# Memory layer of a two-layer decoder step: row maxima read back from device memory, one transpose for both column blocks of the sample, keys' transposes in another PSUM pool

## The chip, the cores and the metric

The kernel runs on one core of one Trainium2 chip, in float32 and in its TensorE form float32r. The metric is the device time of one execution in microseconds (us). Engines are called by the profile's short names: PE is TensorE (PEld its weight load), DVE is VectorE, ACT is ScalarE, POOL is GpSimd, SP is SyncE, which here issues every DMA.

## The reference

One inference step of a trunk of two layers, on a prompt of 256 tokens and a sample of 8 sequences of 8 new tokens, 320 tokens in all, with width 1024. Layer 0 is a spatial-gating MLP, layer 1 an mLSTM (matrix memory) with 8 heads; each is followed by a gated MLP. The change lies in the mLSTM layer. Cut to what matters there, per head:

```python
b = jnp.cumsum(fc, axis=-1)                                   # log forget gates
D = b[..., :, None] - b[..., None, :] + ic[..., None, :]      # masked to s <= t
inter = b + m[..., None]
m_t = jnp.maximum(inter, jnp.max(D, axis=-1))                 # running maximum, one row per head
w_intra, w_inter = jnp.exp(D - m_t[..., None]), jnp.exp(inter - m_t)
sc = jnp.einsum('bhtd,bhsd->bhts', qc, kc) * w_intra
num = w_inter[..., None] * jnp.einsum('bhtd,bhde->bhte', qc, C) + jnp.einsum('bhts,bhse->bhte', sc, vc)
den = w_inter * jnp.einsum('bhtd,bhd->bht', qc, n) + jnp.sum(sc, axis=-1)
h = num / jnp.maximum(jnp.abs(den), jnp.exp(-m_t))[..., None]
...
C_new = decay[..., None, None] * C + jnp.einsum('bhsd,bhse->bhde', kg, vc)
...
hn = ((h - mu) * lax.rsqrt(var + EPS)).reshape(bsz, s, D_B) * gn_g
y = (jax.nn.sigmoid(o_pre) * hn) @ w_out
```

A head has keys and queries of width 128 and values of width 256, that is two blocks of 128 columns.

## The kernel before

Activations lie transposed, with features on the partitions and the 320 tokens along the free dimension. A block of 128 output features is 24 matmuls of 320 columns for a depth of 1024: each weight is split into a rounded high part `wh` and the rest `wl`, the activations likewise, and three of the four products are summed (`chunk`, `block`). A block's 512 KB of weights come by one DMA on SP's queue into a tile `raw` (four buffers, loaded up to four blocks ahead, line 127); ACT casts `wh` (line 154), DVE subtracts to get `wl` (line 155).

**The memory layer** (`layer_b`, from line 635) first makes the gates of all heads (`gates`): per head a row of 392 numbers in `Xf` (320 running maxima, 64 weights of the old state, 8 decays), whose last part is an `Exp` on ACT (line 725). `X` holds the rows as a high part on partitions 0 to 7 and the rest on 32 to 39 (lines 726, 727). Then come the heads in a loop from line 1057. One turn `h` of the loop contains the six weight blocks of head `h` (query, key, two value blocks, two output gate blocks) and, between them, the work of head `h` and the tail of head `h - 1`:

- `inter` and `numer` (h - 1): products with the old state and with the values, into PSUM tiles `num`.
- `stats` (h - 1): mean and variance per token; the normalised result goes to `hn`, three token blocks (128, 128, 64) by 256 columns, one ACT instruction for each.
- `state_prompt`, `state_sample` (h - 1): the new state `C`, with the decays in `dec`, stored from SP.
- `scores` (h): a matmul of `X` with a selector (`sel`, one 128 x 128 matrix for each head) puts head h's row on all 128 partitions, in the PSUM tile `pMb`; ACT makes the weights `w` from it, POOL masks them, DVE makes `Pf`, and from `qw` the operand `Qz`.
- `o_epi` (h): an output gate block is scaled (`o_b`, line 995) and its tanh taken (`th_o`).
- `finish` (h - 1): for each of the two column blocks `e`, three transposes of `hn` into a PSUM tile `phn`, a product with the gate (`y_b`, line 1009), and its split into `yhb` and `ylb`, the operands of the output projection.
- `k_nat`, `v_nat` (h): transposes of keys (`pk`) and values (`pv`) into PSUM, then scaled and split (`kgs`, `kgh`, `kgl`).

Some blocks of the output projection are computed inside the loop (`EARLY_OUT`, turns 4 to 6), the rest after it. After the loop the last head's `numer`, `stats`, two gate blocks and `finish` come, then the remaining projection.

**What sets the order.** PE's instructions are kept in the order of the program (`pin`). The other engines' order, and that of SP's queue, is fixed at build time by the framework's scheduler from the program's order and its own estimates; on the chip each engine runs its list in order. PSUM has eight banks: `psm` with three, which the weight blocks take in turn (with one of the two tiles of `state_sample` in most heads), and `psa` with five for everything else. A tile waits for the readers of the one that held its bank before.

Of the kernel before, what the change touches and what calls it, by code (L numbers as in the profile page):

```python
# [10 lines left out]
F32 = mybir.dt.float32  # L11
# [5 lines left out]
P = 128  # L17
# [8 lines left out]
NH = 8  # L26
# [11 lines left out]
class Net:  # L38
# [596 lines left out]
    def layer_b(self):  # L635
# [5 lines left out]
        with ExitStack() as ctx:  # L641
# [3 lines left out]
            gnh = lp.tile([P, 16], F32, name="gnh")  # L645
            colsT = lp.tile([P, 3, 96], F32, name="cols")
            X = lp.tile([P, 392], F32R, name="X")
            sel = lp.tile([P, NH, P], F32R, name="sel")
            mk = lp.tile([P, NB], F32, name="mk")
            mo = lp.tile([8, 9], F32, name="mo")  # L650
            pads = []
# [9 lines left out]
            def gates(rp):  # L661

                bif = rp.tile([40, 1 + NB], F32, name="bif")
                rst = rp.tile([40, 2, T], F32, name="rst")
                selr = rp.tile([P, NH, P], F32, name="selr")
                RS = rp.tile([P, 384], F32, name="RS")
                nc.sync.dma_start(bif, I["b_if"])
                nc.sync.dma_start(rst, I["seg"])
# [54 lines left out]
                nc.vector.tensor_tensor(seg(wi[:, :64]), m0.unsqueeze(2).to_broadcast([8, NB, NS]), seg(M[:, TP:]), op=SUB)  # L723
                nc.vector.tensor_tensor(wi[:, 64:72], m0, ML, op=SUB)
                nc.scalar.activation(Xf[:, T:392], wi, AF.Exp)
                nc.vector.tensor_copy(X[0:8], Xf)
                nc.vector.tensor_tensor(X[32:40], Xf, X[0:8].bitcast(F32), op=SUB)
                nc.vector.tensor_scalar(gnh, self.vecs[:, V_GN:V_GN + 16], 0.5, None, op0=MULT)
# [54 lines left out]
            def v_epi(h, j, ps):  # L783
# [2 lines left out]
                nc.scalar.copy(vT[:, T:384], ps[:, TP:T])  # L786
                S[h].setdefault("vT", []).append(vT)

            def scores(h):
                s = S[h]  # L790
                q, qh, ql = s["q"]
                k, kh, kl = s["k"]
                pb = self.psa.tile([P, 512], F32, tag="pa", name="pMb")
                sc = self.psa.tile([P, 512], F32, tag="pa", name="psc")
                if h:
                    mm(pb[:, :392], sel[:, h, :], X, True, True)
                mm3(sc[:, :TP], kh, kl, qh, ql, True, True)
                mm(sc[:, TP:384], k[:, P:TP], q[:, P:TP], True, True)
                mm(sc[:, 384:448], k[:, TP:384], q[:, TP:T], True, True)
                if not h:  # L800

                    mm(pb[:, :392], sel[:, h, :], X, True, True)
                w = hp.tile([P, 448], F32, tag="w", name="w", bufs=1)
                for (n, o, c0, c1, t) in ((P, 0, 0, TP, 0), (P, TP, P, TP, 1), (64, 384, TP, T, 2)):
                    nc.scalar.activation(w[:n, o:o + c1 - c0], pb[:n, c0:c1], AF.Exp, scale=-1.0, bias=colsT[:n, t, h:h + 1])
                for o in (0, TP):
                    nc.gpsimd.affine_select(w[:, o:o + P], w[:, o:o + P], pattern=[[1, P]], compare_op=ALU.is_ge, fill=0.0,
                                            base=0, channel_multiplier=-1)
                w3 = seg(w[:64, 384:448])
                nc.gpsimd.affine_select(w3, w3, pattern=[[-NS, NB], [0, NS]], compare_op=ALU.is_ge, fill=0.0, base=0,  # L810
                                        channel_multiplier=1)
                nc.gpsimd.affine_select(w3, w3, pattern=[[NS, NB], [1, NS]], compare_op=ALU.is_ge, fill=0.0, base=0,
                                        channel_multiplier=-1)
                dec = hp.tile([P, NB], F32, tag="dec", name="dec", bufs=2)
                nc.vector.tensor_copy(dec, pb[:, 384:392])
                qw = hp.tile([P, 64], F32, tag="qw", name="qw", bufs=1)
                nc.vector.scalar_tensor_tensor(qw, q[:, TP:T], 0.5, pb[:, T:384], op0=MULT, op1=MULT)
                Qd = Qz.rearrange("p (b e) -> p b e", e=136)
                nc.scalar.copy(Qd[:, :, 0:8], seg(qw))
                nc.vector.tensor_tensor(Qd[:, :, 64:72], seg(qw), Qd[:, :, 0:8].bitcast(F32), op=SUB)  # L820
                Pf = hp.tile([P, 448], F32, tag="Pf", name="Pf", bufs=1)
                Ph = hp.tile([P, 384], F32R, tag="Ph", name="Ph", bufs=1)
                Pl = hp.tile([P, 384], F32R, tag="Pl", name="Pl", bufs=1)
                nc.vector.scalar_tensor_tensor(Pf[:, :384], sc[:, :384], 0.25 * KSC, w[:, :384], op0=MULT, op1=MULT)
                nc.vector.scalar_tensor_tensor(Pf[:64, 384:], sc[:64, 384:448], 0.25 * KSC, w[:64, 384:], op0=MULT, op1=MULT)
                self.split(Ph[:, :384], Pl, Pf[:, :384])
                self.split(Ps[:64, :64], Ps[:64, 64:], Pf[:64, 384:])
                parts = self.parts
                nc.scalar.copy(Ps[64:], Ps[:64])
                self.parts = parts  # L830
                s["P"] = (Ph, Pl, dec)
# [23 lines left out]
            def k_nat(h):  # L855
                s = S[h]
                ks = s["k"][0]
                pk = self.psa.tile([P, 512], F32, tag="pa", name="pk")
                for t in range(3):
                    self.tr(pk[:, t * P:(t + 1) * P], ks[:, t * P:(t + 1) * P], self.ident)  # L860
                kgh = hp.tile([P, 2, P], F32R, tag="kgh", name="kgh", bufs=1)
                kgl = hp.tile([P, 2, P], F32R, tag="kgl", name="kgl", bufs=1)
                kgs = hp.tile([P, 2, P], F32R, tag="kgs", name="kgs", bufs=1)
                kgz = hp.tile([P, NB, P], F32R, tag="kgz", name="kgz", bufs=1)
                g = colsT[:, 2, 32 + h:33 + h]
                src = pk[:, 2 * P:3 * P]

                for i, (r, o) in enumerate(((slice(0, 32), slice(32, 64)), (slice(32, 64), slice(0, 32)))):
                    nc.scalar.activation(kgs[:, i, :], src, AF.Copy, scale=g)
                    nc.vector.scalar_tensor_tensor(kgs[o, i, :], src[r], g[r], kgs[r, i, :].bitcast(F32), op0=MULT, op1=SUB)  # L870
                s["kg"] = (kgh, kgl, kgs, kgz)
                if h < NH - 1:
                    k_mask(h)
                for t in range(2):
                    g = colsT[:, t, 32 + h:33 + h]
                    src = pk[:, t * P:(t + 1) * P]
                    nc.scalar.activation(kgh[:, t, :], src, AF.Copy, scale=g)
                    nc.vector.scalar_tensor_tensor(kgl[:, t, :], src, g, kgh[:, t, :].bitcast(F32), op0=MULT, op1=SUB)
# [52 lines left out]
            def stats(h, between=None):  # L931
# [25 lines left out]
                made = nc.vector.scalar_tensor_tensor(nb, mv[:, :, 0], -1.0, sl, op0=MULT, op1=MULT)  # L957
                if between:
                    self.pin(made)
                for t in range(3):  # L960
                    n = P if t < 2 else 64
                    if h == NH - 1 and t:
                        nc.vector.tensor_scalar(hn[:n, t, :], src[t][:n, :DV], mv[:n, t, 0:1], sl[:n, t:t + 1], op0=SUB, op1=MULT)
                    else:
                        nc.scalar.activation(hn[:n, t, :], src[t][:n, :DV], AF.Identity, scale=sl[:n, t:t + 1], bias=nb[:n, t:t + 1])

            def state_prompt(h):
                s = S[h]
# [24 lines left out]
            def o_epi(h, j, ps):  # L993
                o = lp.tile([P, T], F32, tag="ob", name="o_b", bufs=1)
                nc.vector.tensor_tensor(o, ps[:, :T], self.rb, op=MULT)  # L995
                th = lp.tile([P, T], F32, tag="tho", name="th_o", bufs=4)
                nc.scalar.activation(th, o, AF.Tanh, scale=0.5)
                S[h].setdefault("o", []).append(th)

            def finish(h):  # L1000
                s = S[h]
                yh = hp.tile([P, 2, T], F32R, tag="yhb", name="yhb", bufs=6)
                yl = hp.tile([P, 2, T], F32R, tag="ylb", name="ylb", bufs=6)
                for e in range(2):
                    pt = self.psa.tile([P, 512], F32, tag="pa", name="phn")
                    for t in range(3):
                        self.tr(pt[:, t * P:(t + 1) * P], hn[:, t, e * P:(e + 1) * P], self.ident)
                    y = self.tp.tile([P, T], F32, tag="yf", name="y_b", bufs=2)
                    nc.vector.scalar_tensor_tensor(y, s["o"][e], 1.0, pt[:, :T], op0=ADD, op1=MULT)
                    g = gnh[:, 2 * h + e:2 * h + e + 1]  # L1010
                    nc.scalar.activation(yh[:, e, :], y, AF.Copy, scale=g)
                    nc.vector.scalar_tensor_tensor(yl[:, e, :], y, g, yh[:, e, :].bitcast(F32), op0=MULT, op1=SUB)
# [12 lines left out]
            vb = hp.tile([P, CW], F32R, name="vb")  # L1025
            Qz = hp.tile([P, 8 * 136], F32R, name="Qz")
            Ps = hp.tile([P, P], F32R, name="Ps")
            hn = hp.tile([P, 3, DV], F32, name="hn")
            nc.gpsimd.memset(hn[64:, 2, :], 0.0)
            nc.gpsimd.memset(vh[:, :, DV:DV + 1].bitcast(F32), 1.0)  # L1030
            nc.gpsimd.memset(vh[:, :, DV + 1:].bitcast(F32), 0.0)
            nc.gpsimd.memset(vl[:, :, DV:].bitcast(F32), 0.0)
# [10 lines left out]
            def blk():  # L1043
                return self.block(KD, self.x_rhs)
# [11 lines left out]

            for h in range(NH):
                if h:
                    qk_epi(h, 0, blk())
                    early(h, 0)  # L1060
                    if h == 1:
# [142 lines left out]
def _lay_out(i):  # L1204
# [55 lines left out]
    seg[:, 0, starts] = 0.0  # L1260
    seg[:, 1, starts] = -1e30
    a["seg"] = seg
    sel = np.zeros((P, NH, P), f)
    for h in range(NH):
        sel[h, h] = 1.0
        sel[32 + h, h] = 1.0
    a["sel"] = sel

    b, q = np.arange(NB), s // 32
# [30 lines left out]
```

## Time and profile before

| | before |
|---|---|
| median of 3 runs | 956.08 us (955.75 to 956.54) |
| profiled execution | 956.05 us, span 954.3 us |
| PE matmul busy | 947.3 us (99%) |
| PE weight load busy | 933.8 us (98%) |
| DVE / ACT / POOL busy | 697.3 / 531.9 / 115.8 us |
| memory layer | about 421 to 698 us of the span |
| DMA | 155.19 MB, 163 GB/s |

Matmuls are pipelined, so one's recorded length (309 ns for 320 columns) is longer than the distance to the next one's start; that distance is what it costs. A busy share near 100% says that PE is never waiting long. "idle before" and the arrow in a row name what ended an engine's wait. Times in rows count from the span's start.

### The profile page before, as it was taken

The numbers are of one execution on the slowest core, as the hardware profiler recorded it, in microseconds if no ns is written. First come the engines' busy times: TensorE is split into PE (matmuls) and PEld (weight loads), VectorE is DVE, ScalarE is ACT, GpSimd is POOL, SyncE is SP. The second block draws the span as 40 slices with busy tenths as digits, with TensorE's granted clock in tenths as the row PEclk, the third lists the DMA queues.
The fourth block names the chain that finished last, engine by engine and source line by source line (L and its number), as shares of the span: only waits on it lengthen the run. The fifth ranks groups of instructions, "written<-read, shape, count | busy, mean of one in ns | idle before, by whom it ended". The sixth has DMA issues, their size and how long they took to land.

```text
span 954.3 us, 17131 instructions
## 1 busy us (share of the span) xinstructions
PE 947.3 (99%) x6427; PEld 933.8 (98%) x6427; DVE 697.3 (73%) x1331; ACT 531.9 (56%) x978; POOL 115.8 (12%) x291
## 2 busy tenths in 40 slices
PE   9999999999999999999999999999999999999997
PEld 8889999999999999999999999999999999999997
DVE  6766976577777754559999998788897777775443
ACT  7557543454555443458777876666766445544342
POOL 2200000010000000014333322102102000000000
PEclk9999999999999999999999999999999999999999
DMA  8643346444444465565465655553474444445441
GB/s 270 210 153 133 133 137 198 160 146 147 149 156 155 139 183 147 149 216 175 128 212 175 206 178 196 185 183 118 132 247 148 149 145 154 156 144 155 143 141 56
DMA packets 54214, 155.19 MB, mean 163 GB/s; under 512 B 7372, under 2 KB 11980, under 8 KB 54132
## 3 DMA queue, kind: packets, MB, share of 16 engines
q1 hardware_dynamic: 54132, 154.10, 50.5%
q8 instruction: 51, 0.84, 0.4%
q14 instruction: 31, 0.25, 0.1%
HBM read 142.10 MB, written 11.97 MB: 161 GB/s over the span
## 4 chain that ended last, share of the span: by engine, by line
PE 94%; DVE 3%; ACT 1%; POOL 1%; DMA 0%; issue 0%; SPq 0%; POOLq 0%
PE pm L54 81%; PE pv_a L54 6%; PE num L54 2%; PE pmix L54 1%; PE pcs L54 1%; PE psc L54 1%; PE phn L57 0%; PE pCp L54 0%; DMA raw<-in_a_wv 0%; PE pv L57 0%; DVE wl L155 0%; PE pc L54 0%; DVE bcv L767 0%; PE pg L54 0%; PE pk L57 0%
## 5 line engine op out<-in xcount | busy, mean ns | idle before, releaser
L154 ACT CAST wh<-raw 128x1024 fp32r<-128x1024 f32 (+3 forms) x256 | 257.0, 1004 | 294.1 <-PE pm L54 161.7
L155 DVE TENSOR_TENSOR wl<-raw,wh 128x1024 fp32r<-128x1024 f32 (+3 forms) x256 | 299.0, 1169 | 118.9 <-ACT wh L154 115.0
L54 PE MATMUL pm<-xh,wh 128*128 128x320 f32 x1216 | 372.3, 311 | 0.1
L54 PE MATMUL pm<-xl,wh 128*128 128x320 f32 x1216 | 370.3, 309 | 0.0
L54 PE MATMUL pm<-xh,wl 128*128 128x320 f32 x1216 | 321.2, 309 | 0.0
L54 PEld LDWEIGHTS pm<-xh,wh 128*128 128x128 f32 x1216 | 228.4, 188 | 0.4 <-DVE o_b L995 0.3
L54 PEld LDWEIGHTS pm<-xl,wh 128*128 128x128 f32 x1216 | 228.4, 188 | 0.2
L54 PEld LDWEIGHTS pm<-xh,wl 128*128 128x128 f32 x1216 | 214.5, 188 | 0.0
L54 PE MATMUL pm<-yh_f,wh 128*128 128x320 f32 x352 | 108.8, 309 | 0.0
L54 PE MATMUL pm<-yl_f,wh 128*128 128x320 f32 x352 | 108.8, 309 | 0.0
L54 PE MATMUL pm<-yh_f,wl 128*128 128x320 f32 x352 | 108.8, 309 | 0.0
L54 PEld LDWEIGHTS pm<-yh_f,wh 128*128 128x128 f32 x352 | 66.1, 188 | 0.0
L54 PEld LDWEIGHTS pm<-yl_f,wh 128*128 128x128 f32 x352 | 66.1, 188 | 0.0
L54 PEld LDWEIGHTS pm<-yh_f,wl 128*128 128x128 f32 x352 | 66.1, 188 | 0.0
L531 DVE SCALAR_TENSOR_TENSOR fcv<-fpad,vecs,fcv 128x336 f32<-128x336 f32 x88 | 49.6, 565 | 2.1 <-ACT fcv L529 0.7
L54 PE MATMUL pm<-yh_a,wh 128*128 128x320 f32 x128 | 39.6, 310 | 0.0
L54 PE MATMUL pm<-yh_a,wl 128*128 128x320 f32 x128 | 39.5, 309 | 0.0
L54 PE MATMUL pm<-yl_a,wh 128*128 128x320 f32 x128 | 39.5, 309 | 0.0
L533 ACT ACTIVATE fgl<-fcv 128x256 f32<-128x256 f32 x44 | 18.2, 414 | 37.8 <-DVE fcv L531 37.8
L54 PE MATMUL pm<-yhb,wh 128*128 128x320 f32 x128 | 38.1, 311 | 0.0
L54 PE MATMUL pm<-ylb,wh 128*128 128x320 f32 x128 | 37.8, 309 | 0.0
L303 DVE TENSOR_TENSOR xT<-pm,xT 128x320 f32<-128x320 f32 x39 | 19.1, 489 | 25.1 <-PE pm L54 24.9
(286 smaller groups left out, 1371.7 us busy)
## 6 DMA issues: line engine op xcount, KB each, us to landing
raw<-in_f_up SPq DMA_DIRECT2D x88, 512.0 KB, 3.3
raw<-in_b_win SPq DMA_DIRECT2D x48, 512.0 KB, 4.0
raw<-in_f_dn SPq DMA_DIRECT2D x32, 448.0 KB, 3.3
C<-in_C SPq DMA_DIRECT2D x32, 258.0 KB, 3.7
out_Cs<-C SPq DMA_DIRECT2D x32, 258.0 KB, 2.5
raw<-in_a_win SPq DMA_DIRECT2D x16, 512.0 KB, 3.3
raw<-in_a_wo SPq DMA_DIRECT2D x16, 512.0 KB, 4.3
raw<-in_f_dn SPq DMA_DIRECT2D x16, 512.0 KB, 3.5
```

Of the source, the lines that this page charges most:

```text
L54: self.pin(self.nc.tensor.matmul(out, lhsT, rhs, start=start, stop=stop, skip_group_check=skip))
L154: self.last_split = self.hold(nc.scalar.copy(wh[:, :kn, :], raw[:, :kn, :]))
L155: self.last_low = nc.vector.tensor_tensor(wl[:, :kn, :], raw[:, :kn, :], wh[:, :kn, :].bitcast(F32), op=SUB)
L303: self.nc.vector.tensor_tensor(x, ps[:, :T], x, op=ADD)
L531: nc.vector.scalar_tensor_tensor(cv, pd[:, i:i + NC], self.vec(w + i * KF), cv, op0=MULT, op1=ADD)
L533: nc.scalar.activation(gl[:, :TP], cv[:, :TP], AF.Gelu_apprx_tanh)
```

## The change

- **Rows.** `gates` also writes the eight rows `Xf` to a small tensor in device memory. In turns 1 to 7 a new `rows_in(h)`, the first thing of the turn, reads row h back with a broadcast to 128 partitions, into an SBUF tile `Mb` (two buffers). `scores` takes `Mb` in place of the PSUM tile `pMb`, and the decays straight from it, without the copy `dec`. Head 0 keeps its matmul; the selector holds one matrix instead of eight.
- **Sample's results.** `stats` writes the sample's two column blocks to `hs`, block 0 on partitions 0 to 63 and block 1 on 64 to 127, by two instructions of 64 x 128. `finish` then needs one transpose for both; the prompt's four go into one PSUM tile. The product with the gate is one instruction for the prompt (2 x 256 columns) and one for the sample (2 x 64), into one tile `y_b`; the gate's tanh is one tile for both blocks.
- **Keys' transposes.** `pk` is taken from `psm` in heads 0 to 6, from `psa` in head 7.

```diff
@@ gates
-            sel = lp.tile([P, NH, P], F32R, name="sel")
+            sel = lp.tile([P, P], F32R, name="sel")
...
-                selr = rp.tile([P, NH, P], F32, name="selr")
+                selr = rp.tile([P, P], F32, name="selr")
...
                 nc.scalar.activation(Xf[:, T:392], wi, AF.Exp)
+                nc.sync.dma_start(I["rows"], Xf)
                 nc.vector.tensor_copy(X[0:8], Xf)
@@ scores
+            def rows_in(h):
+                mb = hp.tile([P, 392], F32, tag="Mb", name="Mb", bufs=2)
+                nc.sync.dma_start(mb, I["rows"][h:h + 1, :].to_broadcast([P, 392]))
+                S[h]["rows"] = mb
...
-                pb = self.psa.tile([P, 512], F32, tag="pa", name="pMb")
+                pb = s["rows"] if h else self.psa.tile([P, 512], F32, tag="pa", name="pMb")
                 sc = self.psa.tile([P, 512], F32, tag="pa", name="psc")
-                if h:
-                    mm(pb[:, :392], sel[:, h, :], X, True, True)
...
                 if not h:
-                    mm(pb[:, :392], sel[:, h, :], X, True, True)
+                    mm(pb[:, :392], sel, X, True, True)
...
-                dec = hp.tile([P, NB], F32, tag="dec", name="dec", bufs=2)
-                nc.vector.tensor_copy(dec, pb[:, 384:392])
+                dec = pb[:, 384:392]
+                if not h:
+                    dec = hp.tile([P, NB], F32, name="dec")
+                    nc.vector.tensor_copy(dec, pb[:, 384:392])
@@ k_nat
-                pk = self.psa.tile([P, 512], F32, tag="pa", name="pk")
+                pool, tag = (self.psm, "pm") if h < NH - 1 else (self.psa, "pa")
+                pk = pool.tile([P, 512], F32, tag=tag, name="pk")
@@ stats
-                for t in range(3):
-                    n = P if t < 2 else 64
-                    if h == NH - 1 and t:
-                        nc.vector.tensor_scalar(hn[:n, t, :], src[t][:n, :DV], mv[:n, t, 0:1], sl[:n, t:t + 1], op0=SUB, op1=MULT)
+                last = h == NH - 1
+                for t in range(2):
+                    if last and t:
+                        nc.vector.tensor_scalar(hn[:, t, :], src[t][:, :DV], mv[:, t, 0:1], sl[:, t:t + 1], op0=SUB, op1=MULT)
                     else:
-                        nc.scalar.activation(hn[:n, t, :], src[t][:n, :DV], AF.Identity, scale=sl[:n, t:t + 1], bias=nb[:n, t:t + 1])
+                        nc.scalar.activation(hn[:, t, :], src[t][:, :DV], AF.Identity, scale=sl[:, t:t + 1], bias=nb[:, t:t + 1])
+                for e in range(2):
+                    a, z = hs[64 * e:64 * e + 64, :], ns[:, e * P:(e + 1) * P]
+                    if last:
+                        nc.vector.tensor_scalar(a, z, mv[:64, 2, 0:1], sl[:64, 2:3], op0=SUB, op1=MULT)
+                    else:
+                        nc.scalar.activation(a, z, AF.Identity, scale=sl[:64, 2:3], bias=nb[:64, 2:3])
@@ o_epi
-                th = lp.tile([P, T], F32, tag="tho", name="th_o", bufs=4)
-                nc.scalar.activation(th, o, AF.Tanh, scale=0.5)
-                S[h].setdefault("o", []).append(th)
+                if not j:
+                    S[h]["o"] = lp.tile([P, 2, T], F32, tag="tho", name="th_o", bufs=2)
+                nc.scalar.activation(S[h]["o"][:, j, :], o, AF.Tanh, scale=0.5)
@@ finish
+                pt, ps = [self.psa.tile([P, 512], F32, tag="pa", name="phn") for _ in range(2)]
                 for e in range(2):
-                    pt = self.psa.tile([P, 512], F32, tag="pa", name="phn")
-                    for t in range(3):
-                        self.tr(pt[:, t * P:(t + 1) * P], hn[:, t, e * P:(e + 1) * P], self.ident)
-                    y = self.tp.tile([P, T], F32, tag="yf", name="y_b", bufs=2)
-                    nc.vector.scalar_tensor_tensor(y, s["o"][e], 1.0, pt[:, :T], op0=ADD, op1=MULT)
+                    for t in range(2):
+                        self.tr(pt[:, (2 * e + t) * P:(2 * e + t + 1) * P], hn[:, t, e * P:(e + 1) * P], self.ident)
+                self.tr(ps[:, :P], hs, self.ident)
+                yb = lp.tile([P, 2, T], F32, name="y_b", bufs=1)
+                o = s["o"]
+                for c, n, x in ((slice(0, TP), TP, pt), (slice(TP, T), 64, ps)):
+                    nc.vector.scalar_tensor_tensor(yb[:, :, c], o[:, :, c], 1.0, x[:, :2 * n].rearrange("p (e t) -> p e t", e=2), op0=ADD, op1=MULT)
+                for e in range(2):
+                    y = yb[:, e, :]
                     g = gnh[:, 2 * h + e:2 * h + e + 1]
@@ the loop over heads
-            hn = hp.tile([P, 3, DV], F32, name="hn")
-            nc.gpsimd.memset(hn[64:, 2, :], 0.0)
+            hn = hp.tile([P, 2, DV], F32, name="hn")
+            hs = hp.tile([P, P], F32, name="hs")
...
             for h in range(NH):
                 if h:
+                    rows_in(h)
                     qk_epi(h, 0, blk())
@@ host layout and tensors
-    sel = np.zeros((P, NH, P), f)
-    for h in range(NH):
-        sel[h, h] = 1.0
-        sel[32 + h, h] = 1.0
+    sel = np.zeros((P, P), f)
+    sel[[0, 32]] = 1.0
...
+    I["rows"] = nc.dram_tensor("rows", (NH, 392), F32).ap()
```

## The prediction

> **What bounds the kernel now.** I began with the page's busy times, its share of the chain that ended last, and the time by stages of the memory layer.
>
> ```profile
> PE 947.3 (99%) x6427; PEld 933.8 (98%) x6427; DVE 697.3 (73%) x1331; ACT 531.9 (56%) x978; POOL 115.8 (12%) x291
> PE 94%; DVE 3%; ACT 1%; POOL 1%; DMA 0%; issue 0%; SPq 0%; POOLq 0%
> PE pv L57 <- DVE y_b L1009: 0.6, 1, 0.6
> core 0: us, PE busy (x) PEld busy (x) DVE busy (x) ACT busy (x) POOL busy (x), PEclk, DMA share, GB/s
> 449.00:479.00 30.00, 29.23 (x210) 28.56 (x208) 28.68 (x73) 23.96 (x59) 10.87 (x24) 1.00 0.50 149
> 508.00:536.50 28.50, 28.50 (x209) 28.49 (x208) 26.82 (x66) 21.91 (x51) 10.00 (x13) 1.00 0.59 181
> ```
>
> Matmul and weight load are both near 100%, the chain is PE for 94%, and in the whole kernel PE has one wait for another engine on record, 0.6 us. In head 3 (508.0 to 536.5) PE is never idle, at full clock. So an instruction taken off PE is worth its place in PE's row, as long as nothing new makes PE wait. In head 1 (449 to 479) VectorE is busy 28.68 of 30.00 us and PE waits: there VectorE sets the pace. The changed lines all lie in the memory layer, between 421 and 698 us.
>
> **The row multiply (line 796).** What an instruction costs PE is the distance to the next one's start; the chain of waits, in order of time, gives it (start, length, what; head 7):
>
> ```profile
> 668.15 0.24 PE pcs L54 x2
> 668.39 0.18 PE pMb L54
> 668.57 0.75 PE psc L54 x7
> 669.32 0.66 PE phn L57 x6
> ```
>
> The change drops the `pMb` multiply in heads 1 to 7 (head 0 keeps it) at 0.18 us: 7 x 0.18 = 1.26 us, 1.08 of it in heads 2 to 7.
>
> **The transposes (line 1007).** Six `phn` take 0.66 us, 0.11 each; five remain, in eight heads: 8 x 0.11 = 0.88 us. One of these (head 0's results, transposed during head 1) lies in head 1's stretch, so 7 x 0.11 = 0.77 outside it. The Trainium skill ("TensorE: Matmul & The Clock Gate", Back-to-back issue gap) states about 81 ns for each matmul of 128 columns in a stream of weight load and matmul. By that figure, an estimate, the seven would be worth 0.57 us and the total 0.2 us smaller, at the edge of what can be told from no change; the row of this case, float32 at 110 ns, has a duration and is used.
>
> **Head 1, where PE's saving does not count by itself.** The other 0.29 us (0.18 + 0.11) lie just ahead of this:
>
> ```profile
> 472.19 0.16 DVE L815 COPY dec<-pMb 128x8 f32<-128x8 f32 x1
> 472.26 0.21 DVE L817 SCALAR_TENSOR_TENSOR qw<-qs,pMb 128x64 f32<-128x64 f32 x1
> 472.71 0.56 DVE L824 SCALAR_TENSOR_TENSOR Pf<-psc,w 128x384 f32<-128x384 f32 x1 [0.23 <-POOL w L807]
> 476.37 1.22 DVE L155 TENSOR_TENSOR wl<-raw,wh 128x1024 fp32r<-128x1024 f32 x1
> 477.51 0.48 DVE L995 TENSOR_TENSOR o_b<-pm,rb 128x320 f32<-128x320 f32 x1
> 477.91 0.87 DVE L1009 SCALAR_TENSOR_TENSOR y_b<-th_o,phn 128x320 f32<-128x320 f32 x2
> 478.44 0.44 PE L57 MATMUL pv<-ident,vTb 128*128 128x128 f32 x2 [0.58 <-DVE y_b L1009]
> 478.93 0.36 PE L54 MATMUL num<-Ch,Qz 128*128 128x258 f32 x1
> ```
>
> The small PSUM pool (`psa`, five banks) rotates, and a tile waits for the reader of the one five before it. Now the second `pv` waits for the first `y_b`, and `num` for the second. With `pMb` and `pk` out of that pool, both `pv` fall on tiles read long before, and `num` falls on the prompt's transposes, read by a `y_b` of 512 elements. VectorE is behind there, so `num` starts when VectorE has come that far. Its `y_b` starts 0.07 us earlier without `dec` (472.19 to 472.26), at 477.84; 512 elements take about 0.69 by the rows 0.48 for 320 and 0.56 for 384; `num` follows some 0.1 later: 478.63 against 478.93, 0.30 us gained. Bounds: 0 (VectorE comes no further than now) and 1.14 (the waits gone: 0.58 of idle, 0.27 that the two `pv` from 478.44 to 478.93 take over their 2 x 0.11, and the 0.29). I take 0.30; the 0.23 that `Pf` waited may come on top, since `w` no longer needs PE.
>
> **Keys' transposes in the blocks' pool.** `psm` has three banks. In heads 0 to 6 `pk` now takes a turn, and the next block waits for the read of the block one before it:
>
> ```profile
> 448.74 0.48 DVE L995 TENSOR_TENSOR o_b<-pm,rb 128x320 f32<-128x320 f32 x1
> 448.87 0.39 PE L54 MATMUL pm<-xh,wh 128*128 128x320 f32 x1
> 457.71 0.34 DVE L878 SCALAR_TENSOR_TENSOR kgl<-pk,cols,kgh 128x128 fp32r<-128x128 f32 x1
> 457.11 0.69 DVE L902 TENSOR_TENSOR Cl<-C,Ch 128x516 fp32r<-128x516 f32 x1
> 457.44 0.28 PE L54 MATMUL num<-Ch,Qz 128*128 128x258 f32 x1
> 457.85 0.39 PE L54 MATMUL num<-Cl,Qz 128*128 128x258 f32 x1
> 459.53 0.31 PE L54 MATMUL pm<-xh,wh 128*128 128x320 f32 x1
> 534.45 0.49 DVE L995 TENSOR_TENSOR o_b<-pm,rb 128x320 f32<-128x320 f32 x1 [0.53 <-PE pm L54]
> 536.53 0.31 PE L54 MATMUL pm<-xh,wh 128*128 128x320 f32 x1
> ```
>
> After head 0 this bites: the block that starts at 448.87 must wait for `o_b`, read until 449.22, a loss of about 0.4 us. But at 457.44 PE waits anyway for a `Cl` that VectorE ends at 457.80, 0.41 between two starts where 0.12 is usual (the two `pcs` above: 0.24), and at 478.4 for VectorE again; neither depends on that block's start, so the 0.4 is swallowed. I put it at 0, bounds 0 and +0.4. The third block after `pk` (459.53) needs its last read, 458.05: 1.5 us in hand. In the steady heads `o_b` ends at 534.94 and the block starts at 536.53, 1.6 us in hand; from head 1 to 2, 477.99 against 479.
>
> **Rows through memory.** Out go a write of 12 KB and seven broadcast reads of 196 KB (1.4 MB), in exchange for a selector 0.45 MB smaller.
>
> ```profile
> gB<-in_a_ln_g SPq DMA_DIRECT2D x4, 128.0 KB, 5.0
> L442 SPq DMA_DIRECT2D gB<-in_a_ln_g x4: 477/549/597, 137.8 to 153.0; - x4
> SPq L127 <- DVE wl L155: 610.8, 227, 9.0
> 445.05 0.26 ACT L725 ACTIVATE Xf<-wi 8x72 f32<-8x72 f32 x1
> 446.27 13.33 SPq L127 DMA_DIRECT2D raw<-in_b_win  x4
> 527.89 0.93 ACT L805 ACTIVATE w<-pMb,cols 128x256 f32<-128x256 f32 x3
> 529.49 1.05 ACT L154 CAST wh<-raw 128x1024 fp32r<-128x1024 f32 x1 [0.66 <-ACT w L805]
> ```
>
> The nearest broadcast costs SP's queue 0.55 us to issue and lands after 5.0 us. The read is issued at a head's start (508.0 in head 3) and `w` reads it at 527.9: 19.9 us later, against 9.0 (SP's longest wait for a weight buffer, ahead of it in the queue) + 5.0. The other copy of that buffer was last read by the state updates two heads back, whose own store waits for the same instruction ahead in the queue, so no wait is new there. The write waits for the `Exp` that ends at 445.3, and the weight loads behind it in the queue (446.27) stand four blocks ahead of their use. With DMA shares of 0.50 and 0.59 the added bytes fit. All this: 0 while that cover holds.
>
> **ScalarE and VectorE.** The sample's result becomes two half-width instructions, and `w` and `qw` read SBUF instead of PSUM:
>
> ```profile
> L965 ACT ACTIVATE hn<-num,nb,sl x15: 555/561/567, 469.2 to 684.8; 128x256 f32<-128x256 f32 x15
> L965 ACT ACTIVATE hn<-ns,nb,sl x7: 591/595/595, 470.1 to 667.3; 64x256 f32<-64x256 f32 x7
> ```
>
> From SBUF the same 256 columns cost 595 against 561 ns, so three `w` cost 0.1 us more per head, and the extra `hn` about another 0.1. ScalarE is busy 21.91 of 28.5 us, and the last of these, started at 667.3 and done at 667.9, waits 1.4 us for its transposes (669.32): 0. The selector's copy shrinks to an eighth, with no wait of PE behind it: 0. VectorE's elements in `finish` stay 640.
>
> The last head has less cover, since both halves of `y_b` now need the second gate's tanh (ends 689.1), where the first did not:
>
> ```profile
> 688.64 0.47 ACT L997 ACTIVATE th_o<-o_b 128x320 f32<-128x320 f32 x1 [1.32 <-DVE o_b L995]
> 690.56 0.55 DVE L1012 SCALAR_TENSOR_TENSOR ylb<-y_b,gnh,yhb 128x320 fp32r<-128x320 f32 x1
> 691.63 0.31 PE L54 MATMUL pm<-yhb,wh 128*128 128x320 f32 x1
> 692.08 0.31 PE L54 MATMUL pm<-ylb,wh 128*128 128x320 f32 x1
> ```
>
> The last `ylb` ends at 691.11 and is needed at 692.08, 0.97 in hand; the new order (0.69 + 0.2 for `y_b`, then two `yhb` and `ylb` in turn) ends it near 691.6. I put 0, bounds 0 and +0.3.
>
> **Sum.** -1.08 - 0.77 - 0.30 = -2.15 us. The profiled execution took 956.05 (span 954.3 and 1.75 around it), as good as the median 956.08: 953.9.
>
> **Rivals.**
> (a) *Head 1's wait goes altogether*: 1.14 in place of 0.30, -3.0, 953.05. For it: `w` comes free of PE. Against: VectorE is still 28.6 of 30 us busy.
> (b) *New PSUM waits eat part of the gain.* The 0.4 at 449 and the 0.3 at the end stay, or `o_b` slips in other heads: one 1.22 us split ahead of it, as in head 1, uses up 1.2 of the 1.6 us in hand, a second would cost 0.85 per head. With both bounds 954.6, with one such head 955.5. A page of the Trainium skill ("Perfetto Trace Analysis", Identifying the Most-Contended Engine) says that the same gap repeating on the engine that should be saturated can mean too few SBUF or PSUM buffers. No such repeating gap stands in PE's waits now; this change would be the one to make it.
> (c) *Slower: ScalarE blocked by a late row.* Its instructions run in a fixed order. If `w`, now free of PE, is ordered early in the head, say 5 us in, and SP is held 9.0 us and the row takes 5.0, ScalarE stands for 9 us with the `wh` casts behind it. The cast at 529.49 ends 6 us before its block starts at 536.53, so 3 us of 9 would reach PE. It decides from (2.15 + 1.91) / 7 = 0.58 us per head, a wait of 6.6 us on ScalarE in all seven; at 1 us per head the time is 960.9. Against: `w` stands 20 us into the head today.
> (d) *Saving smaller than the spacing says*, since PE might be held by weight loads (98%) and close the gaps less: at half, 955.
>
> **How the numbers follow.** About 0.2% (1.9 us, 954.2) is what can be told from no change here. Forecast 0.50 and (a) 0.10 are faster: 0.60. (b) 0.22 and (d) 0.06 lie within: 0.28. (c) and several heads of (b) slower: 0.12. The range 952.7 to 955.5 takes in (a), (b) and (d) and leaves out (c).
>
> **What would show it.** Right: no `pMb` after head 0, 40 `phn` instead of 48, heads 2 to 6 shorter by 0.29 us each, PE's only layer wait near 478 on `num` and shorter; a small wait at 448.9 paid back at 457.4. Wrong: `o_b` or `kgl` in front of a block's first matmul in several heads, ScalarE waiting for the rows' DMA, or PE waiting for `ylb` near 692.

## The result and the profile after

The changed kernel takes 963.26 us (962.66 to 965.60, 5 runs) against 956.08 (955.75 to 956.59, 5 runs): a ratio of 1.0079, 95% interval 1.0067 to 1.0090. It is 7.2 us slower, where 2.15 us faster was forecast. Its profiled execution took 962.91 us, its span 960.6 at a granted clock of 0.999.

From the page of the changed kernel, the busy times and the shares of the chain that ended last:

```profile
PE 947.7 (99%) x6412; PEld 932.6 (97%) x6412; DVE 695.1 (72%) x1325; ACT 535.6 (56%) x985; POOL 115.2 (12%) x290
PE 88%; DVE 7%; ACT 2%; issue 1%; POOL 1%; DMA 1%; SPq 0%; DVEq 0%; ACTq 0%; POOLq 0%
```

PE has 15 instructions fewer, as the change says (7 `pMb`, 8 `phn`), and is busy for as long as before: recorded lengths overlap, so this number shows neither the saving nor the loss. The chain does: VectorE's share went from 3 to 7%.

What PE and ScalarE wait for, from the view of waits of the changed kernel (total us, times, longest):

```profile
PE num L54 <- DVE y_b L1027: 4.8, 6, 1.5
PE pm L54 <- DVE o_b L1010: 1.3, 2, 1.2
PE pm L54 <- DVE wl L155: 0.3, 1, 0.3
ACT w L810 <- DMA Mb<-rows: 6.9, 4, 3.0
```

Before, PE had one such wait, 0.6 us on `y_b`. Now `num` waits for `y_b` six times, once in each head from 1 to 6. Head 3 in the timeline of the changed kernel, VectorE's and PE's rows, and below the dots the last head:

```profile
535.91 0.49 DVE L1010 TENSOR_TENSOR o_b<-pm,rb 128x320 f32<-128x320 f32 x1 [0.39 <-PE pm L54]
536.08 0.27 PE L57 MATMUL phn<-ident,hs 128*128 128x128 f32 x1
536.32 1.22 DVE L155 TENSOR_TENSOR wl<-raw,wh 128x1024 fp32r<-128x1024 f32 x1
536.76 0.82 PE L57 MATMUL pv<-ident,vTb 128*128 128x128 f32 x6
537.45 0.88 DVE L1027 SCALAR_TENSOR_TENSOR y_b<-th_o,phn 128x512 f32<-128x512 f32 x2
538.19 0.39 PE L54 MATMUL num<-Ch,Qz 128*128 128x258 f32 x1 [0.61 <-DVE y_b L1027]
538.77 0.31 PE L54 MATMUL pm<-xh,wh 128*128 128x320 f32 x1
...
688.20 0.28 PE L54 MATMUL pCp<-vh,kgl 128*128 128x258 f32 x1
688.65 0.54 DVE L971 TENSOR_SCALAR hn<-num,mv,sl 128x256 f32<-128x256 f32 x1 [0.74 <-POOL sl L961]
689.11 0.48 DVE L1010 TENSOR_TENSOR o_b<-pm,rb 128x320 f32<-128x320 f32 x1
689.64 0.42 PE L54 MATMUL pm<-xh,wh 128*128 128x320 f32 x1 [1.16 <-DVE o_b L1010]
699.75 0.31 PE L54 MATMUL pm<-ylb,wh 128*128 128x320 f32 x1
700.39 0.56 PE L54 MATMUL pm<-yhb,wl 128*128 128x320 f32 x2 [0.33 <-DVE wl L155]
```

The transposes are done, `o_b` is done, and VectorE then splits the next weight block (`wl`, 1.22 us) before it reads the transposes (`y_b`). `num` takes the bank of the prompt's transposes and stands until `y_b` has read it. In the same place before, the timeline has `y_b` right behind `o_b`:

```profile
534.45 0.49 DVE L995 TENSOR_TENSOR o_b<-pm,rb 128x320 f32<-128x320 f32 x1 [0.53 <-PE pm L54]
534.86 0.88 DVE L1009 SCALAR_TENSOR_TENSOR y_b<-th_o,phn 128x320 f32<-128x320 f32 x2
535.40 0.82 PE L57 MATMUL pv<-ident,vTb 128*128 128x128 f32 x6
535.98 0.37 PE L54 MATMUL num<-Ch,Qz 128*128 128x258 f32 x1
536.53 0.31 PE L54 MATMUL pm<-xh,wh 128*128 128x320 f32 x1
```

The order on VectorE's list was changed by the edit, in all of heads 1 to 6. The lower rows of the first of these two fences are the last head: there `o_b` stands behind an `hn` that waits for POOL, and PE goes from 688.20 to 689.64, 1.44 where 0.12 is usual; a second gap follows at 699.75, 0.64 where 0.15 is usual.

Where the time lies can be read from one tile. The rows of `pv` run from head 0 to head 7; each gives the first and last start:

```profile
L57 PE MATMUL pv<-ident,vTb x48: 272/273/328, 448.3 to 674.7; 128*128 128x128 f32 x48
```
```profile
L57 PE MATMUL pv<-ident,vTb x48: 272/272/273, 448.2 to 679.1; 128*128 128x128 f32 x48
```

Seven heads took 226.4 us before and 230.9 after, +4.5. From the last `pv` to the end of the span it is 279.6 before (954.3 - 674.7) and 281.5 after, +1.9: the last head. Taken as the excess of each distance between two starts on PE over its usual value, the six waits of `num` cost 1.63 us in head 1, 1.02 in head 4 and 0.77 in each of the other four, 5.7 in all; the last head 1.32 + 0.49, where 0.21 stood before; 0.67 at 472 (order around `C` and `Cl`) and 0.38 at 561 (a wait for ScalarE's `vTb`) are new. Against it stand the 7 x 0.18 + 8 x 0.11 = 2.14 us of PE's work and 0.96 of head 1's old waits at 478. Compared with the same place before, a wait costs a little more than its excess: from the first `pv` to the next block's first matmul it is 1.13 us before (535.40 to 536.53) and 2.01 in the change (536.76 to 538.77), +0.88, since `num` used to follow the last `pv` after 0.03. That adds about 0.1 in each of heads 2 to 6.

### The profile page after: what moved, and what is told of

The parts are those of the page before. It is cut to its first block, busy times and chain, and to the rows that moved or that the text cites. A ratio compares the mean times of both kernels' runs of the same rounds, so it can differ in the third digit from the quotient of the medians.

```text
span 960.6 us, 17098 instructions
## 1 busy us (share of the span) xinstructions
PE 947.7 (99%) x6412; PEld 932.6 (97%) x6412; DVE 695.1 (72%) x1325; ACT 535.6 (56%) x985; POOL 115.2 (12%) x290
## 4 chain that ended last, share of the span: by engine, by line
PE 88%; DVE 7%; ACT 2%; issue 1%; POOL 1%; DMA 1%; SPq 0%; DVEq 0%; ACTq 0%; POOLq 0%
PE pm L54 77%; PE pv_a L54 6%; PE num L54 2%; DVE wl L155 2%; PE pmix L54 1%; DVE C L1005 1%; POOL sl L961 1%; DMA Mb<-rows 1%; DVE Cl L910 0%; PE pcs L54 0%; ACT wh L154 0%; DVE y_b L1027 0%; PE psc L54 0%; PE pCp L54 0%; PE pc L54 0%
```

## The experiments

Two theories were open after the comparison. **Order**: the one transpose for the sample puts `y_b` behind a weight split on VectorE, and that alone makes the loss. **Rows**: reading the maxima through memory holds ScalarE (6.9 us of waits), and PE follows. A run's ratio is to executions of the kernel before, measured together with it; "layer" is the distance from the first `pv` of head 0 to the last of head 7.

### Each part by itself

e1, the rows alone (the diff's part "Rows", the rest as before):

```diff
+                nc.sync.dma_start(I["rows"], Xf)
...
-                pb = self.psa.tile([P, 512], F32, tag="pa", name="pMb")
+                pb = s["rows"] if h else self.psa.tile([P, 512], F32, tag="pa", name="pMb")
...
+                    rows_in(h)
```

> Only the rows through memory (no pMb multiply after head 0); transposes and PSUM pools as before. Theory (order: the loss comes from the sample part, which moves a weight split ahead of y_b in VectorE's list): in this kernel's list y_b follows o_b directly, so PE has no wait in heads 2 to 6; PE saves 7 x 0.18 = 1.26 us, of which up to 1.0 us may go at the last head, where hn now precedes o_b: 954.8 to 956.3. Rival (pools: a wait in the PSUM rotation whatever the order): 954.8, since the pool is only relieved. Rival (late rows block ScalarE and with it the casts): 960 or more.

e2, the sample's results alone:

```diff
+                self.tr(ps[:, :P], hs, self.ident)
...
+                for c, n, x in ((slice(0, TP), TP, pt), (slice(TP, T), 64, ps)):
+                    nc.vector.scalar_tensor_tensor(yb[:, :, c], o[:, :, c], 1.0, x[:, :2 * n].rearrange("p (e t) -> p e t", e=2), op0=ADD, op1=MULT)
```

> Only the sample's part (one transpose for both blocks, y_b for the prompt and for the sample, one tanh tile); the row multiply and the pools as before. Order: 960 to 963, with a wait of 0.8 to 1.7 us on PE before pv or num in each of heads 1 to 6, behind y_b, against 0.88 us saved. Pools: 955.2 (0.88 us saved, keys' transposes still in the small pool). Late rows: 955.2.

e3, the keys' transposes alone:

```diff
-                pk = self.psa.tile([P, 512], F32, tag="pa", name="pk")
+                pool, tag = (self.psm, "pm") if h < NH - 1 else (self.psa, "pa")
+                pk = pool.tile([P, 512], F32, tag=tag, name="pk")
```

> Only the keys' transposes moved to the blocks' pool. Order: 956.1 within 0.5, with a wait of 0.3 to 0.4 us at the first block of head 1 that is paid back later in that head. Pools: the whole loss, 961 or more. Late rows: 956.1.

Measured: e1 956.73 us, ratio 1.0003 (0.9994 to 1.0012); e2 964.33, 1.0084 (1.0069 to 1.0099); e3 955.70, 0.9995 (0.9986 to 1.0004). Alone, the sample's part loses as much as the whole change, and neither of the others loses anything, though ScalarE's waits for rows are in e1 too (3.8 us). PE's waits in e2, from the view of waits:

```profile
PE pv L57 <- DVE y_b L1019: 6.4, 6, 2.3
```

With `pMb` and `pk` still in the five banks, the tile that meets the late `y_b` is `pv`, and the wait is longer than in the whole change (some 1.0 us per head in place of 0.77). Whether the other two parts soften this one is not shown. The spans of the profiled executions are 963.1 and 960.6, but in e2's the granted clock was 0.5 from 479.7 to 483.1, right behind PE's longest wait (2.28 us, head 1): matmuls of 320 columns stood 0.27 us apart there in place of 0.15, some 1.4 us in all, an estimate from these distances. Two of e2's four executions have a mean clock of 0.997 and spans of 963.1 and 963.4; the other two, at 0.999 and 1.0, have 961.4 and 961.5, inside the 960.6 to 962.0 of the changed kernel. I had expected 960 to 963 for e2 and had not counted on the clock; these two took 963.4 and 963.5 us.

e1 did not keep the 1.26 us of `pMb` either (its range ended at 956.3): it gave them back at three places (0.70 at 683.6, where 0.21 stood before, 0.63 at 677.0, 0.44 at 472), all of them waits for VectorE. Two of the changed kernel's gaps belong here and not to the sample's part. In the last head `hn` stands ahead of `o_b` in e1, in the change and in e5 (0.70, 1.32, 1.32), all with rows from memory, and not in e2 and e10, which have none (0.30, 0.29); e6, with rows and three banks, has it not either (0.28). The wait at 472 (0.44 to 0.77) is in every run with the rows and in none without.

### The order forced on the kernel before

e4 is the kernel before with one thing altered: for the results of heads 0 to 5, finished in turns 1 to 6, the first `y_b` is ordered behind the next weight split, which for this is written earlier in the program (`prefetch`).

```diff
+                    with ExitStack() as late:
+                        if h < NH - 2 and not e:
+                            self.prefetch(0, self.used + 3)
+                            late.enter_context(self.tc.issue_after(self.last_low.ins))
-                    nc.vector.scalar_tensor_tensor(y, s["o"][e], 1.0, pt[:, :T], op0=ADD, op1=MULT)
+                        nc.vector.scalar_tensor_tensor(y, s["o"][e], 1.0, pt[:, :T], op0=ADD, op1=MULT)
```

> The kernel before with one thing changed: in heads 1 to 6 one more weight split (1.22 us on VectorE) is ordered ahead of y_b; nothing else is moved on PE or between pools. Order: y_b comes 1.2 us later where it had about 0.25 us in hand, so PE waits some 1.0 us before pv and num in each of six heads: 961 to 963. Pools and late rows: 956.1 within 0.5.

Measured 963.96 us (962.28 to 964.29), ratio 1.0075 (1.0058 to 1.0092), 1.0 above the end of the expected range. Its PE waits, and VectorE in head 3:

```profile
PE pv L57 <- DVE y_b L1013: 4.3, 6, 1.7
...
538.01 0.49 DVE L995 TENSOR_TENSOR o_b<-pm,rb 128x320 f32<-128x320 f32 x1 [0.79 <-PE pm L54]
538.42 1.21 DVE L155 TENSOR_TENSOR wl<-raw,wh 128x1024 fp32r<-128x1024 f32 x1
539.56 0.88 DVE L1013 SCALAR_TENSOR_TENSOR y_b<-th_o,phn 128x320 f32<-128x320 f32 x2
```

This one order, with no other part of the change, makes as large a loss. The scheduler moved a few instructions more behind it, for example a `Cl` ahead of a split, as it did in e2; but in the memory layer PE's waits on record are on `y_b` alone. That is what "order" claims.

### The change with the order given back

e5 is the changed kernel with the sample's transpose and its `y_b` first. Number, size and banks of everything stay.

```diff
+                self.tr(ps[:, :P], hs, self.ident)
                 for e in range(2):
...
-                self.tr(ps[:, :P], hs, self.ident)
...
-                for c, n, x in ((slice(0, TP), TP, pt), (slice(TP, T), 64, ps)):
+                for c, n, x in ((slice(TP, T), 64, ps), (slice(0, TP), TP, pt)):
```

> The changed kernel with one order turned round: the sample's one transpose and its y_b come ahead of the prompt's four transposes and y_b. Same instructions, same banks. Order: a y_b is ready after one transpose instead of four, so the list has no split between o_b and y_b in heads 1 to 6; the five steady waits of 0.88 us go (4.4) and head 1's 1.7 shrinks to some 0.6, while the last head (o_b behind hn, 1.3 us) and head 1's 0.7 near 472 stay: 957.0 to 958.5. Rival (the bank: num lies on the prompt's transposes now, and their one long y_b is what it waits for): the wait stays within 0.2 us, 962 to 963.5.

e6 takes three banks: each column block of the prompt has its own, with a `y_b` of 256 elements each, and the sample follows.

```diff
+                pts = [self.psa.tile([P, 512], F32, tag="pa", name="phn") for _ in range(3)]
...
+                for e in range(2):
+                    nc.vector.scalar_tensor_tensor(yb[:, e, :TP], o[:, e, :TP], 1.0, pts[e][:, :TP], op0=ADD, op1=MULT)
```

> The changed kernel with the prompt's transposes in one bank for each column block and a y_b for each (256 columns), the sample's in a third: y_b is three instructions, PE's work is that of the changed kernel. Order: y_b is ready after two transposes, no split ahead of it; in the last head o_b again stands ahead of hn in VectorE's list and the first y_b does not wait for the second gate's tanh, which takes back about 1.1 and 0.5 us there: 955.5 to 957. Rival (bank): still one wait per head, 960 or more.

Measured: e5 957.52 us, 1.0014 (1.0005 to 1.0023); e6 957.21, 1.0012 (1.0003 to 1.0021), 0.2 above its range: in its last head the first wait fell to 0.28, but the second grew to 1.04, on a `wl`. Head 3 in e5's timeline, `y_b` again right behind `o_b`, with both of its instructions in one row:

```profile
534.38 0.48 DVE L1010 TENSOR_TENSOR o_b<-pm,rb 128x320 f32<-128x320 f32 x1
534.78 0.87 DVE L1027 SCALAR_TENSOR_TENSOR y_b<-th_o,phn 128x128 f32<-128x128 f32 x2
534.81 0.82 PE L57 MATMUL pv<-ident,vTb 128*128 128x128 f32 x6
535.39 0.36 PE L54 MATMUL num<-Ch,Qz 128*128 128x258 f32 x1
```

`num` starts 0.58 after the first of the six `pv`, with no wait on record, against 1.43 in the changed kernel (536.76 to 538.19). 5.7 of the 7.2 us are back, though the buffers are the same: the gap that repeated in every head came from an order, not from too few banks. The Trainium skill ("Perfetto Trace Analysis", Optimization Strategy) says that a gap repeating on the engine that should be saturated can mean too few SBUF or PSUM buffers. This case's traces do not bear that reading out: the gap of 0.77 us went in e5 with the same buffers.

Why the framework's scheduler moved the split can be argued, and isn't shown: by its own estimates the prompt's `y_b`, now behind four transposes and one more instead of three, isn't ready when `o_b` ends, and the split is. That both e5 (one transpose ahead of the first `y_b`) and e6 (two) restore the old order agrees with it.

e7 is e6 with `Cl` ordered behind `C` in head 1, for the 0.67 at 472:

```diff
+                        if h == 1:
+                            late.enter_context(tc.issue_after(self.c_made.ins))
+                        for i in (0, 1):
+                            state_split(h, i)
```

> As the run with three banks, and in head 1 the two splits of the old state (Cl) are put behind the state update of the head before (C) in VectorE's list. Order: the 0.7 us near 472 go, of which a part is only moved to the wait behind y_b in the same head: 0.2 to 0.7 us less than with three banks alone. If head 1 is paced by VectorE's total work whatever its order: no change against three banks alone.

957.72 us, 1.0015 (1.0007 to 1.0024), no gain. In its trace the wait at 472 became one of 0.77 for ScalarE's `vTb`, and three of 0.74 to 0.84 stand later, between 530 and 566, one of which (0.73 at 564) e6 has too. The profiled execution took 959.96 us, 2.2 above e7's median, so these sizes do not stand for its other executions.

### The last head and the rows

e8 is e5 with the last head finished as before, and its `hn` ordered behind `o_b`:

```diff
+                if h == NH - 1:
+                    with tc.issue_after(self.o_made.ins):
+                        for t in range(3):
...
+                if h == NH - 1:
+                    for e in range(2):
+                        pt = self.psa.tile([P, 512], F32, tag="pa", name="phn")
```

> The changed kernel with the sample's transpose and y_b first (as in the run sample-first), and the last head finished the old way: three token blocks, six transposes, a y_b per column block, and its hn put behind o_b in VectorE's list. Theory (order): the last head's waits (1.3 before the second gate block, 0.5 before the first finished output block) fall back to 0.2 and 0, for 0.11 of an added transpose: 1.3 to 1.7 us less than sample-first, 955.8 to 956.3. Rival (the last head's wait is only PE running ahead of ScalarE's chain, and moves elsewhere): within 0.5 of sample-first, 957 to 958.

e9 is e8 with each row read one head earlier (a third buffer, the tile `X` that head 0 has done with):

```diff
-                mb = hp.tile([P, 392], F32, tag="Mb", name="Mb", bufs=2)
+                mb = hp.tile([P, 392], F32, tag="Mb", name="Mb", bufs=2) if h % 3 else X.bitcast(F32)
...
-                    rows_in(h)
+                    for i in (1, 2) if h == 1 else (h + 1,) if h < NH - 1 else ():
+                        rows_in(i)
```

> As the run with the last head the old way, and each row is read back one head earlier, with X as a third buffer. Late rows: ScalarE's waits for rows (6.6 us in sample-first) vanish, and with them the waits that the delayed list passes on to VectorE and PE (0.8 to 1.0 us in heads 3 and 4), and the spread between runs narrows: 954.5 to 955.4. If ScalarE's cover is enough, as predicted: no change within 0.3.

e10 is e5 without the rows part (the matmul `pMb` and the large selector are back), to ask whether the rows are worth having:

```diff
-                pb = s["rows"] if h else self.psa.tile([P, 512], F32, tag="pa", name="pMb")
+                pb = self.psa.tile([P, 512], F32, tag="pa", name="pMb")
...
+                if h:
+                    mm(pb[:, :392], sel[:, h, :], X, True, True)
```

> The changed kernel, sample first, without the rows through memory: the selector multiply pMb and dec as before. PE does 1.26 us more than sample-first, ScalarE waits for no row, and o_b stands ahead of hn in the last head. If the rows gain nothing net in the changed kernel: 955.2 to 956.2, below sample-first (957.5). If PE's 1.26 us are won: 958 or more.

Measured: e8 956.29 us, 0.9997 (0.9989 to 1.0006); **e9 954.21** (953.53 to 955.04), **0.9979 (0.9970 to 0.9988)**; e10 956.50, 1.0002 (0.9993 to 1.0010). e9 beats both kernels, by 2.1 us (0.2%) the one before, and is 0.3 below the expected range. e8 is 1.2 below e5: the last head's gaps of 1.32 and 0.49 are gone but for 0.21. What e9 then removes is ScalarE's waits for rows, which e8 has as the change has them:

```profile
ACT w L810 <- DMA Mb<-rows: 6.5, 4, 2.4
```

In the changed kernel's timeline one of them, and the read's issue on SP's queue behind a store:

```profile
539.64 0.39 SPq L1006 DMA_DIRECT2D out_Cs<-C  x1
540.07 0.42 SPq L793 DMA_DIRECT2D Mb<-rows  x1
545.12 0.51 ACT L810 ACTIVATE w<-Mb,cols 128x256 f32<-128x256 f32 x1 [1.81 <-DMA Mb<-rows]
```

`w` has been ordered 6 us into the head (the last `pv` of the head before starts at 537.3), not 20, and so in heads 3 to 7; the reads land 3.7 to 6.7 us after their issue, by the view of the tile `Mb`:

```profile
DMA to landing us min/median/max: 3.7/4.7/6.7
```

e9 has no such wait. Its edit moved an order as well: in heads 3 to 7 `w` now stands 6 to 11 us ahead of the head's start on ScalarE's list, so the 2.1 us are the worth of the early read and of that order together. What is left of PE's waits in the layer is this, from e9's view of waits, with its row of `pv` and its chain:

```profile
PE pcs L54 <- DVE C L1014: 0.3, 1, 0.3
PE pm L54 <- DVE o_b L1019: 0.2, 1, 0.2
```
```profile
L57 PE MATMUL pv<-ident,vTb x48: 272/273/273, 447.8 to 672.3; 128*128 128x128 f32 x48
```
```profile
PE 95%; DVE 2%; ACT 1%; issue 1%; DMA 0%; POOL 0%; SPq 0%; ACTq 0%
```

The layer takes 224.5 us there, 1.9 less than before. Each head from 2 to 6 is shorter by 0.30 to 0.38 us (by the last `pv` of each), where 0.29 had been worked out. e10 lands 0.3 above what was expected if the rows gain nothing: head 1's wait (0.65 at 477.6, where 0.96 stood), 0.63 at 668 and 0.49 at 694 eat the transposes' 0.88. e9 is 2.3 below e10, of which the last head, finished another way, makes about 0.7 (0.29 + 0.49 there in e10, none in e9, less one transpose). So the rows look worth their place once nothing waits for them, by some 1.6 us; no run alters them alone in e9.

e11 is the changed kernel with the same early reads and nothing else (e9's diff on the change), since both causes could add up or hide each other:

> The changed kernel with nothing altered but this: each row of maxima is read one head earlier. In e9 the same edit was worth 2.1 us, but there the waits on y_b had been removed first. Theory A (the losses add up: ScalarE's waits for the rows delay PE wherever they occur): about 961.2, 2.1 below the changed kernel's 963.3. Theory B (in the changed kernel the pace of heads 1 to 6 is set by VectorE's wait for the transposes, and ScalarE's lateness hides behind it): 962.8 to 963.3, and the waits of num on y_b grow or stay. In both, ScalarE's waits for the rows are gone from the trace.

962.38 us (961.29 to 964.00), 1.0064 (1.0050 to 1.0078): 0.9 below the change, where e9 gained 2.1 over e8 by the same edit. Its PE waits:

```profile
PE num L54 <- DVE y_b L1027: 4.5, 6, 1.5
```

Between the two expectations, nearer to "hidden": the rows' late landing makes up to 0.9 of the loss (the gap of 0.38 at 561 is gone and head 4's wait is 0.25 shorter; the intervals of the two ratios overlap), and the waits on `y_b` stand.

### Does head 0's bank wait cost anything?

e12 is e9 with `pk` of head 0 back among the five banks; the order on every engine is the same.

```diff
-                pool, tag = (self.psm, "pm") if h < NH - 1 else (self.psa, "pa")
+                pool, tag = (self.psm, "pm") if 0 < h < NH - 1 else (self.psa, "pa")
```

> e9 with the keys' transposes of head 0 alone back in the pool of five banks; the order on every engine is otherwise the same. The stall of 0.33 us near 448.4 must vanish. If it is absorbed later (as the prediction had it for the changed kernel, where num waited at 457.4 anyway): 954.2, no change, and a wait of num on Cl appears near 457. If nothing downstream absorbs it: 953.9.

954.39 us (953.55 to 955.13), 0.9980 (0.9971 to 0.9989). First e9's timeline, then e12's:

```profile
448.82 0.41 PE L54 MATMUL pm<-xh,wh 128*128 128x320 f32 x1 [0.17 <-DVE o_b L1019]
...
457.40 0.28 PE L54 MATMUL num<-Ch,Qz 128*128 128x258 f32 x1
457.51 0.28 PE L54 MATMUL num<-Cl,Qz 128*128 128x258 f32 x1
```
```profile
448.93 0.39 PE L54 MATMUL pm<-xh,wh 128*128 128x320 f32 x1
...
457.50 0.28 PE L54 MATMUL num<-Ch,Qz 128*128 128x258 f32 x1
457.91 0.39 PE L54 MATMUL num<-Cl,Qz 128*128 128x258 f32 x1
```

The wait at 448.8 is gone and its size comes back at 457.5 (0.41 between two starts in place of 0.11). The stall is swallowed.

## Why the prediction was wrong

**The step that failed** is in "ScalarE and VectorE": "VectorE's elements in `finish` stay 640", entered at nothing. The elements do stay, but the step took VectorE's list for fixed, with `y_b` right behind `o_b`; the same assumption stands in head 1's step, where `num` was to follow `y_b` at 478.63. With a first `y_b` that depends on four transposes in place of three, a 1.22 us split was ordered ahead of it, in six heads. e2 (that part alone: +8.2 us, part of it a lower clock), e4 (that order forced: +7.9) and e5 (that order undone: 5.7 back) show it. Rival (b) had the nearest mechanism: a second split in a head's reach, priced at 0.85 per head against 0.77 measured as an excess, 0.88 against the same stretch before. It counted `o_b` alone as the instruction that could slip, and put several such heads into the 0.12 for slower.

**The last head**, put at 0 with a bound of +0.3, cost 1.6 (1.32 + 0.49 - 0.21). The bound came from the length of the new chain behind the second tanh; what decided was again an order, `o_b` behind `hn`, which waits for POOL's `sl`, and a `wl` behind other work at 699.9. About 1.0 of it came from two parts together: the rows put `hn` ahead of `o_b` (1.32 in e5, 0.29 in e10, which is e5 without them). The prediction priced the sample's part alone at this place.

**Rows through memory** was put at 0 "while that cover holds". The cover of 19.9 us did not hold: `w`, which no longer needs PE, came 6 us into the head in heads 3 to 7. That is rival (c) in its place but not in its price: four waits of 6.9 us in all, the longest 3.0, not seven of 9. Reading the rows earlier gave back up to 0.9 us in the change (e11) and 2.1 where nothing hid them (e8 to e9), in both with `w` moved on ScalarE's list, and by themselves (e1) the rows made nothing slower.

**What held.** PE's terms (0.18 for a `pMb`, 0.11 for a transpose): e9, which has the change's PE work in all heads but the last and no split ahead of `y_b`, gained 2.1 us. The price of `pk` in the blocks' pool: a stall of 0.33 for the 0.4 forecast, swallowed at 457.4 as worked out (e3 within no change, e12). Head 1's wait at 478 did go in e5 and e9, all but 0.2, as rival (a) had it, but 0.67 at 472 came in its place, since `Cl` of both halves now stands ahead of `C`. The net gain in e9 was 0.2 for the 0.30 forecast: 0.11 between the last `pv` of head 0 and that of head 1 (29.76 to 29.65), 0.11 from there to `num` (0.32 to 0.21). That it comes near the forecast is luck, since two effects outside the forecast's working nearly cancel. `w` from SBUF costs ScalarE 25 ns more (507 against 482 for 256 columns), where 34 was used.

**Left open**: why the scheduler's estimate changed the order is argued, and no run looked at it by itself. Of the 6.3 us by which the span grew, the excesses named, less the savings, come to 5.3; the 0.1 more in each of heads 2 to 6 makes 5.8, and about 0.5 lies in distances too small to name one by one.

## What to carry to other kernels

Where a scheduler fixes the order of an engine's list at build time, an edit that joins two instructions or makes one depend on more also moves others: price it as if the longest independent instruction of that engine (here 1.22 us) went ahead of it, and ask who holds a PSUM bank meanwhile. If a gap then repeats in every turn of a loop, look for the instruction that changed places before adding buffers; giving it an earlier first part (the small `y_b` first) can restore the order at no cost. A load whose reader has been freed of its old dependence has lost its cover as well, so issue it a turn earlier, and look where the scheduler then puts the reader.

## What the runs showed of the hardware

Halving an ACT instruction hardly shortens it. From the groups of before and of the change, 64 x 256 in one instruction and 64 x 128 in two, all from the SBUF tile `ns`:

```profile
L965 ACT ACTIVATE hn<-ns,nb,sl 64x256 f32<-64x256 f32 x7 | 4.2, 594 | 0.0
```
```profile
L980 ACT ACTIVATE hs<-ns,nb,sl 64x128 f32<-64x128 f32 x14 | 6.8, 489 | 0.1
```

Two halves take 978 ns in place of 594, +0.38 per head where the prediction had "another 0.1"; ScalarE had the room, so no run shows a cost. On VectorE the split was cheap: 677 + 277 ns for 512 + 128 elements against 2 x 478 for 320 (groups of `y_b`).

In one trace PE's clock fell behind a wait. These are the stretches around head 1's wait in e2 (start and end, PE, its weight load, VectorE, ScalarE, POOL, then the granted clock, the DMA share and GB/s), with the wait itself:

```profile
476.00:480.00 4.00, 1.72 (x15) 1.48 (x14) 4.00 (x8) 2.26 (x6) 0.00 (x0) 0.96 0.93 280
480.00:484.00 4.00, 4.00 (x20) 4.00 (x20) 3.84 (x10) 2.99 (x7) 1.80 (x2) 0.62 0.69 205
479.82 0.69 PE L57 MATMUL pv<-ident,vTb 128*128 128x128 f32 x2 [2.28 <-DVE y_b L1019]
```

The clock was 1.0 up to the wait and again from 483.1 on. In the trace of e4, whose longest wait is 1.7 us, and in that of the change (1.5), no such stretch stands in the layer. No run shows what sets it; by their mean clock, it is in two of e2's four executions.
